# Order of products and placement of operands at the turn into a Strassen-Winograd up projection

## The chip, the cores and the metric

The kernel runs on one core of one Trainium2 chip. The metric is device time in microseconds, the median of three runs; a profile of one further execution tells where the time lies.

## The reference

Two layers of a hybrid encoder over 16 meta tokens and 1024 frames, width 1024. The change lies between the output projection of the attention half and the gated feed-forward that follows it:

```python
h = h + jnp.concatenate([o_gla, o_fox], axis=-1) @ w_out[i]
h = h + conv_ffn(rms_norm(h, ffn_norm[i]), w_up[i], conv_w[i], conv_b[i], w_down[i])

def conv_ffn(x, w_up, conv_w, conv_b, w_down):
    h = x @ w_up                       # 1040 x 1024 by 1024 x 5632
    hp = jnp.pad(h, ((0, 0), (CONV_W - 1, 0), (0, 0)))
    hc = conv_b
    for j in range(CONV_W):            # causal depthwise conv of width 3
        hc = hc + hp[:, j:j + L] * conv_w[j]
    u, g = jnp.split(hc, 2, axis=-1)
    return (jax.nn.silu(g) * u) @ w_down
```

## The kernel before

Everything is fp32 to the accuracy of a split: each operand is a high part `hi` (cast by ScalarE to the matmul's rounded fp32) and a low part `lo` (the rest, by VectorE), and `mm3` issues three matmuls for each pair of blocks, on lines L216, L217 and L218: hi by hi, lo by hi, hi by lo. Activations are transposed: 128 features on the partitions, tokens along the row. Tokens are taken in two halves of 520 (layer 0) or 516 and 8 more (layer 1), `sl[0]` and `sl[1]`, each as two chunks of 260 or 258 columns.

`ffn_up` does the output projection and the up projection. In the first, `wout` runs over the eight feature blocks m for half 0 and then for half 1: matmuls into one of four two-bank PSUM tiles, the residual add on VectorE (L1095), a store of the result to `hm` from GpSimd's queue (L1096), a square on ScalarE (L1101) and its sum into `acc` (L1102). After the second block of half 1, `scale(0)` turns the sum of half 0 into the norm's factor (a matmul with ones into `ssq`, then L1074, two ScalarE activations in `rsqrt`, L273 to L275), and `first_operand(k)` scales and splits block k of half 0 (L1079, and L1037 and L1038 in `put`); the table `turn` says after which block of half 1 which k are done.

The up projection multiplies each of 22 pairs j (128 columns of u, 128 of g) by the Strassen-Winograd scheme: features 0 to 511 and 512 to 1023 and the two halves of tokens form a 2 by 2 block problem with seven products p. A product is four k-blocks by two chunks by three matmuls, 24 in all. Products 1 and 2 use the first operands (k 0 to 3, and k 4 to 7) and need only half 0. Product 6 needs the operand T2, 7 needs T3, 4 needs N4, 5 needs T1, and 3 the fourth block itself; these are made from the residual stream, `dd`, and the norm's factor of half 1 by `make_t23`, `make_n4`, `make_t1` and `make_b22`, which the table `before` calls ahead of the i-th product of the order `seq`. Their sums are on VectorE (L1132, L1133, L1151) and GpSimd (L1144, L1152). `seq` starts with products 1 and 2 of pairs 0, 1 and 2, then runs 6, 7, 4, 5, 3 of pairs 0 and 1 alternately, and from pair 2 on one pair at a time.

On the weight side, `up_operand` loads the four half tiles A11, A12 (buffers `raw`, four of them, shared with the output projection) and A21, A22 (buffers `raw2`, seven) on SP's queue (L991; L983 for the first two products of pair 2), and VectorE combines them (L997): S1 = A21 + A22, S2 = S1 - A11, A21 = A11 - A21, A12 = A12 - S2. `up_split` casts (L1013) and subtracts (L1014). `ensure(i)` keeps the weights four products ahead (`AHEAD`).

In PSUM, product 1 lies in bank p0, p1 or p3 for pairs 0, 1 and 2, product 2 in p2 for all three; products 6, 7 and 4 go on accumulating in the bank of product 1. `evacuate` copies a bank out by ScalarE (L1181) or adds it by VectorE to what is there (L1180); after product 3 come the convolution (L1169, L1173), SiLU, the product of both (L1202) and a store from GpSimd's queue (L1203).

TensorE runs in the order in which the program is written (`manual_schedule`). The other engines' and queues' orders are fixed when the program is built, by a planner that takes what is ready by its own costs, the earliest traced first; each engine then runs its list in order. A buffer is taken again when its last reader is done.

Of the kernel before, what the change touches and what calls it, by code (L numbers as in the profile page):

```python
# [10 lines left out]
F32 = mybir.dt.float32  # L11
# [3 lines left out]
ALU = mybir.AluOpType  # L15
# [33 lines left out]
HALVES, HALVES_LAST = (0, 520, 520), (8, 524, 516)  # L49
AHEAD = 4  # L50
NSPLIT = 4


class Slots:
# [6 lines left out]
    def add(self, pool, n, prefix):  # L61
        ids = [(pool, f"{prefix}{i}") for i in range(n)]
        self.free += ids
        return ids
# [68 lines left out]
class Kern:  # L133
# [845 lines left out]
    def up_operand(self, lyr, j, p, fw, raws, odd):  # L979
        nc = self.nc  # L980
        if j == 2 and p in (1, 2):
            src = fw.tile([128, 4, 128], F32, tag="raw2", name="raw2")
            nc.sync.dma_start(src[:], self.wm[lyr, M_UP + 4][:, 4 * p - 4:4 * p, :])  # L983
            return self.up_split(src, fw, odd)
        if j not in raws:
            u, g = self.wm[lyr, M_UP + 2 * j], self.wm[lyr, M_UP + 2 * j + 1]
            q = raws[j] = {}
            for name, src, k0, own in (("A11", u, 0, True), ("A21", g, 0, False), ("A22", g, 4, False), ("A12", u, 4, True)):
                q[name] = self.wp.tile([128, 4, 128], F32, tag="raw", name="raw", bufs=4) if own else \
                    fw.tile([128, 4, 128], F32, tag="raw2", name="raw2")  # L990
                nc.sync.dma_start(q[name][:], src[:, k0:k0 + 4, :])  # L991
        q = raws[j]

        def combine(out, a, b, op):
            if out not in q:
                q[out] = fw.tile([128, 4, 128], F32, tag="raw2", name="raw2")
            nc.vector.tensor_tensor(out=q[out][:], in0=q[a][:], in1=q[b][:], op=op)  # L997
        if p == 6:
            combine("S1", "A21", "A22", ALU.add)
            combine("S2", "S1", "A11", ALU.subtract)  # L1000
        elif p == 7:
            combine("A21", "A11", "A21", ALU.subtract)
        elif p == 3:
            combine("A12", "A12", "S2", ALU.subtract)
        src = q[{1: "A11", 2: "A12", 3: "A12", 4: "A22", 5: "S1", 6: "S2", 7: "A21"}[p]]
        return self.up_split(src, fw, odd)
# [10 lines left out]
    def ffn_up(self, lyr, mix, hT, pp, fw, halves, o0, during_last):  # L1017
        nc, s = self.nc, self.slots
        W = halves[2]
        n = W // 2  # L1020
        sl = [slice(c, c + W) for c in halves[:2]]
        gain = lambda k: self.v(lyr, V_FN, k)
        bank2 = lambda name, i: pp.tile([128, 2, 512], F32, tag=f"p{i}", name=name, bufs=1)
        used = lambda ps: ps[:, :, :n]
        two = lambda ap: ap.rearrange("p (a b) -> p a b", b=n)
# [6 lines left out]
        def operand(x):  # L1032
            X[x] = [[s.get(F32R, f"x{x}", (128, 2, 520)) for _ in range(2)] for _ in range(2)]

        def put(x, k, src, lo=None):
            hi_, lo_ = (X[x][i][k // 2].t[:, k % 2, :W] for i in range(2))
            nc.scalar.copy(hi_, src)  # L1037
            (lo or nc.vector).tensor_tensor(out=lo_, in0=src, in1=hi_.bitcast(F32), op=ALU.subtract)  # L1038

        seq = [(j, p) for j in range(3) for p in (1, 2)] + [(j, p) for p in (6, 7, 4, 5, 3) for j in range(2)]
        seq += [(2, 6), (2, 5), (2, 7), (3, 1), (2, 4), (2, 3)]
        for j in range(3, NFF - 1):
            seq += [(j, 2), (j, 6), (j, 5), (j, 7), (j + 1, 1), (j, 4), (j, 3)]
# [15 lines left out]
        acc, sq = s.get(F32, "r"), half_slot("sq")  # L1061
# [15 lines left out]
        def first_operand(k):  # L1077
            h = hT[k][:, sl[0]]
            nc.vector.scalar_tensor_tensor(out=h, in0=h, scalar=gain(k), in1=acc[:, sl[0]], op0=ALU.mult, op1=ALU.mult)  # L1079
            put(1 + k // 4, k % 4, h)  # L1080
        turn = {1: (), 3: (0, 1), 4: (2,), 5: (3, 4), 6: (5,), 7: (6, 7)}

        def wout(i, h):
            m = orders[h][i]
            k0 = KD - 1 if m < NSPLIT else 0

            def f(w):
                if h == 1 and i == KD - 1:
                    ensure(0)
                ps = bank2("wo", i % 4)  # L1090
                for k in range(len(w)):
                    for c in range(2):
                        self.mm3(ps[:, c, :n], w[k], mix[k0 + k], halves[h] + c * n, n, k == 0, k == len(w) - 1)
                x = hT[m][:, sl[h]]
                nc.vector.tensor_tensor(out=two(x), in0=used(ps), in1=two(x), op=ALU.add)  # L1095
                nc.gpsimd.dma_start(self.hm[m][:, sl[h]], x)  # L1096
                if i == 0:
                    nc.scalar.activation(acc[:, sl[h]], x, AF.Square)
                else:
                    t = half(sq, i % 2)  # L1100
                    nc.scalar.activation(t, x, AF.Square)  # L1101
                    (nc.vector if h and i > 5 else nc.gpsimd).tensor_tensor(out=acc[:, sl[h]], in0=acc[:, sl[h]], in1=t, op=ALU.add)  # L1102
                if h == 0:
                    return
                if m < NSPLIT:
                    nc.scalar.mul(half(gt, m % 2), x, gain(m))
                else:
                    nc.vector.scalar_tensor_tensor(out=diff(m - 4), in0=x, scalar=gain(m), in1=half(gt, m % 2),
                                                   op0=ALU.mult, op1=ALU.subtract)
                if i == 1:  # L1110
                    scale(0)
                    operand(1)
                    operand(2)
                for k in turn.get(i, ()):
                    first_operand(k)
            return (self.wm[lyr, M_WO + m][:, k0:KD, :], f)
# [5 lines left out]
        lowk, highk, t0, t1 = hT[:4], hT[4:], sl[0], sl[1]  # L1122
# [2 lines left out]
            scale(1)  # L1125
            s.put(sq, *tmp)

        def make_t23():
            operand(6)
            for k in range(4):  # L1130
                x, y = diff(k), lowk[k][:, t0]
                nc.vector.tensor_tensor(out=x, in0=x, in1=acc[:, t1], op=ALU.mult)  # L1132
                nc.vector.tensor_tensor(out=y, in0=x, in1=y, op=ALU.add)  # L1133
                put(6, k, y)
            operand(7)
            for k in range(4):
                put(7, k, diff(k))
            s.put(*dd)

        def make_n4():  # L1140
            operand(4)
            for k in range(4):
                x = highk[k][:, t0]
                nc.gpsimd.tensor_tensor(out=x, in0=x, in1=lowk[k][:, t0], op=ALU.subtract)  # L1144
                put(4, k, x)

        def make_t1():
            operand(5)
            for k in range(4):
                x, y = highk[k][:, t1], lowk[k][:, t0]  # L1150
                nc.vector.scalar_tensor_tensor(out=x, in0=x, scalar=gain(4 + k), in1=acc[:, t1], op0=ALU.mult, op1=ALU.mult)  # L1151
                nc.gpsimd.tensor_tensor(out=y, in0=x, in1=y, op=ALU.subtract)  # L1152
                put(5, k, y)
            s.put(acc, *lowk)

        def make_b22():
            operand(3)
            for k in range(4):
                put(3, k, highk[k][:, t1])
            s.put(*highk)  # L1160
        before = {1: second_half, 2: make_t23, 7: make_n4, 9: make_t1, 12: make_b22}


        st = {}
# [13 lines left out]
        def evacuate(j, p):  # L1178
            q = st[j]
            add = lambda out, ps: nc.vector.tensor_tensor(out=two(out), in0=used(ps), in1=two(out), op=ALU.add)  # L1180
            copy = lambda out: nc.scalar.copy(two(out), used(q["a"]))  # L1181
            if p == 1:
                q["u"] = s.get(F32, "hu")
                copy(q["u"][:, t0])
            elif p == 6:
                copy(q["u"][:, t1])
            elif p == 7:
                q["g"] = s.get(F32, "hg")
                copy(q["g"][:, t1])
            elif p == 4:  # L1190
                copy(q["g"][:, t0])
            elif p == 2:
                add(q["u"][:, t0], q["y"])
            elif p == 3:
                add(q["u"][:, t1], q["x"])
                u, g = conv(q["u"], j), conv(q["g"], j + NFF)
                uo, go = u[:, o0:T], g[:, o0:T]
                nc.scalar.activation(go, go, AF.Silu)
                if j == NFF - 1:
                    self.preload = self.tc.keep_in_program_order(  # L1200
                        nc.scalar.preload_act_table_set("natural_log_exp_and_others"))
                nc.vector.tensor_tensor(out=uo, in0=uo, in1=go, op=ALU.mult)  # L1202
                nc.gpsimd.dma_start(self.actd[j][:, o0:T], uo)  # L1203
                s.put(u, g)
                del st[j]
            q.setdefault("done", set()).add(p)
            if p in (5, 7) and {5, 7} <= q["done"]:
                add(q["g"][:, t1], q["x"])

        for i, (j, p) in enumerate(seq):  # L1210
# [3 lines left out]
            q = st.setdefault(j, {})  # L1214
            bank, first = {2: "y", 5: "x", 3: "x"}.get(p, "a"), p in (1, 2, 5)
# [218 lines left out]
```

## Time and profile before

| | us |
|---|---|
| Runs | 2645.58, 2647.34, 3453.82 (median 2647.34) |
| Profiled execution | 2645.09 |
| its span | 2643.3 |
| TensorE busy | 2523.9 (95%) |
| VectorE busy | 1759.9 (67%) |
| ScalarE busy | 1240.1 (47%) |
| GpSimd busy | 457.9 (17%) |
| mean granted clock of TensorE | 0.987 |

In the profile PE is TensorE, PEld its weight loads, DVE VectorE, ACT ScalarE, POOL GpSimd, SP SyncE. A group's row has the line, engine, operation, tiles written and read, shapes and count, then busy time and mean nanoseconds of one, then the engine's idle time ahead of them and what ended it. A row of a timeline has start, length, the instruction, and in brackets the idle time before it with its releaser. Where several equal instructions follow each other, the row has them together. A window's row ends with the granted clock of TensorE, the mean busy share of the DMA engines, and GB/s. Output and up projection of layer 0 run from 550 us on, those of layer 1 from 1859 us on.

### The profile page before, as it was taken

To read this page: it belongs to the slowest core of one execution; us is meant where nothing else is said; L and a number is where in the kernel's file an instruction comes from. 1 tells how busy PE (TensorE), PEld (TensorE's weight loads), DVE (VectorE), ACT (ScalarE), POOL (GpSimd) and SP (SyncE) were. 2 spreads that over 40 slices of the span, in tenths; PEclk is the share of its full clock that TensorE was granted. 3 is DMA by queue.
4 is the path that set the end of the run, shared out by engine and by line. 5 is a ranking of instruction groups with operands and counts; after the bars stand their busy time and mean duration, and the time that the engine had idled before them with its cause. 6 is when DMAs were issued, how large, how long until landed. Compare 5 with 4: busy or idle time off the path is not lost.

```text
span 2643.3 us, 46336 instructions
## 1 busy us (share of the span) xinstructions
PE 2523.9 (95%) x18102; PEld 2407.2 (91%) x18102; DVE 1759.9 (67%) x3484; ACT 1240.1 (47%) x2677; POOL 457.9 (17%) x596
## 2 busy tenths in 40 slices
PE   8999999897999999999999999998989999999997
PEld 7988898897999999999999888887889999998886
DVE  7655676759877777643665666666698767776335
ACT  6345665645544445421343565665455444453112
POOL 4033333333000000000201333332320000000002
PEclk9999999998999999999999999999999999999999
DMA  3222124341222222632312222142512222245222
GB/s 125 65 83 70 47 83 124 106 131 58 97 81 76 85 77 92 217 94 58 103 56 65 75 72 74 56 138 91 158 51 85 83 81 77 83 139 189 65 55 77
DMA packets 114476, 240.72 MB, mean 91 GB/s; under 512 B 14432, under 2 KB 36192, under 8 KB 114256
## 3 DMA queue, kind: packets, MB, share of 16 engines
q1 hardware_dynamic: 96000, 182.27, 22.7%
q0 software_dynamic: 16384, 53.18, 5.5%
q8 instruction: 142, 2.33, 0.4%
q10 hardware_dynamic: 1872, 2.31, 0.2%
q14 instruction: 78, 0.64, 0.1%
HBM read 174.01 MB, written 50.91 MB: 85 GB/s over the span
## 4 chain that ended last, share of the span: by engine, by line
PE 77%; DVE 13%; ACT 4%; issue 3%; DMA 2%; POOL 2%; DVEq 0%; SPq 0%; POOLq 0%; ACTq 0%
PE mm L216 12%; PE mm L217 12%; PE mm L218 12%; PE up L216 10%; PE up L217 10%; PE up L218 10%; PE av L706 2%; PE tr L688 2%; DVE S L655 1%; DVE x L1038 1%; PE wo L217 1%; PE wo L216 1%; PE wo L218 1%; DVE PT L331 1%; ACT P L667 1%
## 5 line engine op out<-in xcount | busy, mean ns | idle before, releaser
L216 PE MATMUL up<-x,hi 128*128 128x260 f32 (+1 forms) x2464 | 701.3, 285 | 22.7 <-DVE hu L1180 20.3
L217 PE MATMUL up<-x,lo 128*128 128x260 f32 (+1 forms) x2464 | 699.2, 284 | 0.0
L218 PE MATMUL up<-x,hi 128*128 128x260 f32 (+1 forms) x2464 | 698.5, 283 | 0.0
L216 PEld LDWEIGHTS up<-x,hi 128*128 128x128 f32 x2464 | 467.5, 190 | 24.4 <-DVE hu L1180 20.7
L217 PEld LDWEIGHTS up<-x,lo 128*128 128x128 f32 x2464 | 467.9, 190 | 0.1
L218 PEld LDWEIGHTS up<-x,hi 128*128 128x128 f32 x2464 | 467.8, 190 | 0.0
L216 PE MATMUL mm<-xh,hi 128*128 128x348 f32 (+4 forms) x1056 | 365.1, 346 | 0.0
L218 PE MATMUL mm<-xl,hi 128*128 128x348 f32 (+4 forms) x1056 | 340.9, 323 | 0.0
L217 PE MATMUL mm<-xh,lo 128*128 128x348 f32 (+4 forms) x1056 | 340.8, 323 | 0.0
L1014 DVE TENSOR_TENSOR lo<-raw,hi 128x512 fp32r<-128x512 f32 x308 | 212.9, 694 | 146.2 <-ACT hi L1013 146.2
L183 ACT CAST hi<-raw 128x512 fp32r<-128x512 f32 (+1 forms) x264 | 142.3, 543 | 329.8 <-PE mm L218 240.0
L217 PE MATMUL mm<-ah,lo 128*128 128x400 f32 (+1 forms) x760 | 266.4, 351 | 0.2 <-DVE lo L185 0.2
L218 PE MATMUL mm<-al,hi 128*128 128x400 f32 (+1 forms) x760 | 265.9, 350 | 0.0
L216 PE MATMUL mm<-ah,hi 128*128 128x400 f32 (+1 forms) x760 | 265.8, 350 | 0.0
L185 DVE TENSOR_TENSOR lo<-raw,hi 128x512 fp32r<-128x512 f32 (+1 forms) x196 | 120.7, 620 | 181.1 <-ACT hi L183 177.5
L1013 ACT CAST hi<-raw 128x512 fp32r<-128x512 f32 x308 | 190.3, 620 | 107.6 <-PE up L218 92.7
L216 PEld LDWEIGHTS mm<-xh,hi 128*128 128x128 f32 x1056 | 201.0, 190 | 6.0 <-issue 5.3
L217 PEld LDWEIGHTS mm<-xh,lo 128*128 128x128 f32 x1056 | 200.9, 190 | 0.4 <-issue 0.3
L218 PEld LDWEIGHTS mm<-xl,hi 128*128 128x128 f32 x1056 | 199.9, 189 | 0.4 <-issue 0.3
L1203 POOL DMA_DIRECT2D actd<-cv x44 | 23.4, 533 | 830.0 <-DVE cv L1202 830.0
L667 ACT ACTIVATE P<-S,m 116x460 f32<-116x460 f32 (+2 forms) x224 | 124.8, 561 | 76.9 <-DVE m L655 72.6
L331 DVE TENSOR_TENSOR PT<-tr,PT 116x464 fp32r<-116x464 f32 (+3 forms) x240 | 122.1, 516 | 55.8 <-ACT PT L330 54.1
(248 smaller groups left out, 5269.0 us busy)
## 6 DMA issues: line engine op xcount, KB each, us to landing
raw<-in_wm_dram SPq DMA_DIRECT2D x328, 256.0 KB, 2.6
raw<-in_wd_dram SPq DMA_DIRECT2D x64, 256.0 KB, 2.6
actd<-cv POOLq DMA_DIRECT2D x22, 520.0 KB, 2.9
st<-actd SPq DMA_DIRECT2D x22, 520.0 KB, 4.9
actd<-cv POOLq DMA_DIRECT2D x22, 512.0 KB, 3.0
st<-actd SPq DMA_DIRECT2D x22, 512.0 KB, 4.8
cb<-cd SPq DMA_DIRECT2D x16, 520.0 KB, 4.2
kA<-kA SPq DMA_DIRECT2D x24, 260.0 KB, 3.8
```

The lines of the kernel that those rows point to most:

```text
L183: nc.scalar.copy(hi[:, :n, :], raw[:, :n, :])
L185: eng.tensor_tensor(out=lo[:, :n, :], in0=raw[:, :n, :], in1=hi[:, :n, :].bitcast(F32), op=ALU.subtract)
L216: nc.tensor.matmul(ps, wh, xh[:, c0:c0 + n], start=first, stop=False, skip_group_check=more)
L217: nc.tensor.matmul(ps, wl, xh[:, c0:c0 + n], start=False, stop=False, skip_group_check=more)
L218: nc.tensor.matmul(ps, wh, xl[:, c0:c0 + n], start=False, stop=last, skip_group_check=more)
L331: nc.vector.tensor_tensor(out=lo, in0=src, in1=hi.bitcast(F32), op=ALU.subtract)
L655: nc.vector.tensor_tensor_reduce(out=S[:rows, :n], in0=S[:rows, :n], in1=cb[:rows, c0:k1], scale=1.0, scalar=(BIG if ci == 0 else m[:rows, ...
L667: nc.scalar.activation(P[:rows, :n], S[:rows, :n], AF.Exp, scale=-1.0, bias=m[:rows, nch - 1:nch], accum_out=(den if nch == 1 else d3[:row ...
L688: nc.tensor.transpose(tr[:w, j, :rows], P[:rows, o:o + w], id_)
L706: nc.tensor.matmul(av[:, a:width], w.rearrange("p a b -> p (a b)"), x, start=(t == 0 and i == 0), stop=(t == last and i == 1))
L1013: nc.scalar.copy(hi[:], src[:])
L1014: nc.vector.tensor_tensor(out=lo[:], in0=src[:], in1=hi[:].bitcast(F32), op=ALU.subtract)
```

## The change

- In the first three pairs product 2 comes before product 1. The first product of a pair is copied to `u` by ScalarE, the second is added to it by VectorE. For pairs 3 to 21 the order stays.
- `turn` makes the first operands of k 4 to 7 before those of k 0 to 3.
- `make_t23` is parted: T2 stays at its place, behind the scale of half 1; T3 is traced ahead of the eighth product, N4 one product later than it was, T1 one product later too.
- The sums of squares (L1102) and the subtractions for N4 and T1 (L1144, L1152) are on VectorE in all cases.
- For pairs 0 to 4, S1 is not added by VectorE: A21's half tile is loaded once more into a `raw2` buffer of its own on SP's queue, as soon as the pair's tiles are, and a DMA from GpSimd's queue adds A22's half to it.

```diff
+N_DMA_SUM = 5
...
                 nc.sync.dma_start(q[name][:], src[:, k0:k0 + 4, :])
+            if j < N_DMA_SUM:
+                q["S1"] = fw.tile([128, 4, 128], F32, tag="raw2", name="raw2")
+                nc.sync.dma_start(q["S1"][:], g[:, 0:4, :])
+                nc.gpsimd.dma_start(q["S1"][:], g[:, 4:8, :], accum_op=ALU.add)
...
-            combine("S1", "A21", "A22", ALU.add)
+            if "S1" not in q:
+                combine("S1", "A21", "A22", ALU.add)
...
-        seq = [(j, p) for j in range(3) for p in (1, 2)] + [(j, p) for p in (6, 7, 4, 5, 3) for j in range(2)]
+        seq = [(j, p) for j in range(3) for p in (2, 1)] + [(j, p) for p in (6, 7, 4, 5, 3) for j in range(2)]
...
-        turn = {1: (), 3: (0, 1), 4: (2,), 5: (3, 4), 6: (5,), 7: (6, 7)}
+        turn = {1: (), 3: (4, 5), 4: (6,), 5: (7, 0), 6: (1,), 7: (2, 3)}
...
-                    (nc.vector if h and i > 5 else nc.gpsimd).tensor_tensor(out=acc[:, sl[h]], in0=acc[:, sl[h]], in1=t, op=ALU.add)
+                    nc.vector.tensor_tensor(out=acc[:, sl[h]], in0=acc[:, sl[h]], in1=t, op=ALU.add)
...
-        def make_t23():
+        def make_t2():
...
+        def make_t3():
             operand(7)
...
-                nc.gpsimd.tensor_tensor(out=x, in0=x, in1=lowk[k][:, t0], op=ALU.subtract)
+                nc.vector.tensor_tensor(out=x, in0=x, in1=lowk[k][:, t0], op=ALU.subtract)
...
-                nc.gpsimd.tensor_tensor(out=y, in0=x, in1=y, op=ALU.subtract)
+                nc.vector.tensor_tensor(out=y, in0=x, in1=y, op=ALU.subtract)
...
-        before = {1: second_half, 2: make_t23, 7: make_n4, 9: make_t1, 12: make_b22}
+        before = {1: second_half, 2: make_t2, 7: make_t3, 8: make_n4, 10: make_t1, 12: make_b22}
...
-            copy = lambda out: nc.scalar.copy(two(out), used(q["a"]))
-            if p == 1:
-                q["u"] = s.get(F32, "hu")
-                copy(q["u"][:, t0])
+            copy = lambda out, bank="a": nc.scalar.copy(two(out), used(q[bank]))
+            if p in (1, 2):
+                bank = "a" if p == 1 else "y"
+                if "u" in q:
+                    add(q["u"][:, t0], q[bank])
+                else:
+                    q["u"] = s.get(F32, "hu")
+                    copy(q["u"][:, t0], bank)
...
-            elif p == 2:
-                add(q["u"][:, t0], q["y"])
```

## The prediction

> **What bounds the kernel now.** I read the page first, then TensorE's waits around the two turns from the output projection into the up projection (layer 0 near 550 to 700 us, layer 1 near 1910 to 2060), then the stages by windows, then the timelines of VectorE, ScalarE and GpSimd inside the turn of layer 0.
>
> ```profile
> span 2643.3 us, 46336 instructions
> ...
> PE 2523.9 (95%) x18102; PEld 2407.2 (91%) x18102; DVE 1759.9 (67%) x3484; ACT 1240.1 (47%) x2677; POOL 457.9 (17%) x596
> ...
> L216 PE MATMUL up<-x,hi 128*128 128x260 f32 (+1 forms) x2464 | 701.3, 285 | 22.7 <-DVE hu L1180 20.3
> ```
>
> TensorE idles 22.7 us in front of the up products, 20.3 of it behind VectorE's evacuation L1180. TensorE's waits name the places, the first three lines in layer 0, the last in layer 1:
>
> ```profile
> PE up L216 <- DVE hu L1180: 10.2, 1, 10.2
> PE wo L217 <- DVE lo L185: 2.1, 1, 2.1
> PE wo L216 <- ACT hi L183: 1.7, 1, 1.7
> ...
> PE up L216 <- DVE hu L1180: 10.0, 1, 10.0
> ```
>
> So there is one stall of 10 us per layer. Its neighbourhood by windows (columns: length, then busy time and count of PE, PEld, DVE, ACT, POOL, then granted clock, DMA share, GB/s):
>
> ```profile
> 601.70:612.50 10.80, 8.65 (x48) 8.45 (x49) 9.20 (x14) 5.47 (x10) 3.60 (x3) 0.68 0.28 98
> 612.50:628.30 15.80, 15.70 (x126) 15.20 (x125) 14.28 (x23) 7.82 (x14) 3.54 (x3) 1.00 0.10 35
> 628.30:638.40 10.10, 0.00 (x0) 0.00 (x0) 8.98 (x12) 6.09 (x11) 4.36 (x3) 0.61 0.00 1
> 638.40:644.10 5.70, 5.64 (x26) 5.64 (x27) 4.87 (x10) 1.18 (x3) 0.00 (x0) 0.50 0.35 99
> 644.10:668.40 24.30, 23.25 (x192) 22.92 (x191) 24.27 (x33) 12.32 (x22) 6.72 (x4) 1.00 0.20 64
> ...
> 690.00:1068.00 378.00, 378.00 (x3155) 377.80 (x3154) 282.55 (x358) 188.75 (x269) 10.10 (x19) 1.00 0.27 90
> ```
>
> A product is 24 matmuls; 378 us over 3155 gives 0.120 us each, 2.88 us a product. Five products (120 matmuls and a norm sum) end by 628.3. Then come 10.1 us of nothing, and the sixth, product 2 of pair 2, needs 5.7 us because the clock is at 0.50: the stall costs 10.1 + 2.8. The next 192 matmuls, eight products, end at 668.4, where product 3 of pair 0 begins. From 690 on TensorE is full. VectorE is full as well, but only in the turn:
>
> ```profile
> 578.00:704.00 126.00, 109.48 (x845) 107.31 (x844) 116.56 (x159) 67.69 (x110) 32.46 (x27) 0.92 0.27 90
> ...
> 704.00:1068.00 364.00, 364.00 (x3038) 363.80 (x3038) 268.86 (x340) 181.68 (x260) 9.57 (x18) 1.00 0.27 89
> ```
>
> VectorE: 93% busy from 578 to 704, 74% after. Its timeline shows why the evacuation was late:
>
> ```profile
> 622.08 0.70 DVE L275 SCALAR_TENSOR_TENSOR r<-nt 128x520 f32<-128x520 f32 x1
> 622.69 0.69 DVE L997 TENSOR_TENSOR raw<-raw,raw 128x512 f32<-128x512 f32 x1
> 623.30 1.31 DVE L1132 TENSOR_TENSOR dd<-dd,r 128x520 f32<-128x520 f32 x2
> ...
> 626.35 0.69 DVE L1038 TENSOR_TENSOR x<-h,x 128x520 fp32r<-128x520 f32 x1
> 629.42 0.70 DVE L1038 TENSOR_TENSOR x<-h,x 128x520 fp32r<-128x520 f32 x1 [2.38 <-ACT x L1037]
> ...
> 637.71 0.69 DVE L1180 TENSOR_TENSOR hu<-up,hu 128x520 f32<-128x520 f32 x1
> 638.32 0.68 DVE L1014 TENSOR_TENSOR lo<-raw,hi 128x512 fp32r<-128x512 f32 x1
> 638.92 1.28 DVE L997 TENSOR_TENSOR raw<-raw,raw 128x512 f32<-128x512 f32 x2
> ```
>
> L1180 of product 2 of pair 1 (its matmuls ended by 625.4) stands in the queue behind T2 and T3 and runs at 637.71; bank p2 is free then and no sooner. In the middle VectorE idles 2.38 us for a ScalarE cast which itself sits behind GpSimd's subtraction:
>
> ```profile
> 628.24 1.15 ACT L1037 CAST x<-h 128x520 fp32r<-128x520 f32 x2 [2.36 <-POOL h L1144]
> ```
>
> **The change, part by part.** Instructions first. Two VectorE operations in a row take 1.31 us and one 0.70, so one more in a row costs 0.61.
>
> (a) *Product 2 ahead of product 1.* Product 2 now fills bank p2 and ScalarE copies it out; the add on VectorE is of product 1, in banks 0, 1 and 3, which product 6 of the same pair needs next. The three p2 products wait for copies (0.59 us, and ScalarE idles here), so the 10.1 us wait at the sixth product goes, with its half clock. Six products and the norm sum end at 628.3 + 2.9 = 631.2 and not 644.1: 12.9 us earlier. What is late next: product 6 of pair 0 needs T2, its weights S2, and the add of product 1.
>
> (b) *T2 alone.* r is ready at 622.8 (L275). T2 is 12 operations of VectorE, 7.3 us, and a cast of 0.62: about 631, plus three others that fall in between (a weight split, S2, one add), 1.8: 632.8 for the fourth piece, which product 6 wants at 631.2 + 2.2 = 633.4. No stall, or one of about 1 us. T3 and N4 stand behind and have one product and three products more.
>
> (c) *No arithmetic on GpSimd.* Twelve sums of squares and eight subtractions per layer move to VectorE. GpSimd's groups, and VectorE's own in the turn (mean ns last before the bar):
>
> ```profile
> L1102 POOL TENSOR_TENSOR r<-r,sq 128x520 f32<-128x520 f32 x12 | 18.7, 1554 | 1.7 <-ACT sq L1101 1.4
> ...
> L1144 POOL TENSOR_TENSOR h<-h,h 128x520 f32<-128x520 f32 x4 | 7.4, 1848 | 14.4 <-DVE h L1133 14.4
> L1152 POOL TENSOR_TENSOR h<-h,h 128x520 f32<-128x520 f32 x4 | 6.7, 1702 | 14.1 <-DVE h L1151 14.1
> ...
> L1038 DVE TENSOR_TENSOR x<-h,x 128x520 fp32r<-128x520 f32 x18 | 13.2, 752 | 2.4 <-ACT x L1037 2.4
> L1014 DVE TENSOR_TENSOR lo<-raw,hi 128x512 fp32r<-128x512 f32 x15 | 11.3, 758 | 0.0
> L997 DVE TENSOR_TENSOR raw<-raw,raw 128x512 f32<-128x512 f32 x14 | 10.2, 762 | 0.0
> L1038 DVE TENSOR_TENSOR x<-dd,x 128x520 fp32r<-128x520 f32 x4 | 4.9, 1233 | 0.0
> L1151 DVE SCALAR_TENSOR_TENSOR h<-h,vec,r 128x520 f32<-128x520 f32 x4 | 3.9, 1016 | 0.0
> L1132 DVE TENSOR_TENSOR dd<-dd,r 128x520 f32<-128x520 f32 x4 | 2.7, 698 | 0.0
> ```
>
> Where GpSimd computes, VectorE's operations of 0.70 us are stretched: against the 698 ns of L1132 (which ran with GpSimd idle) L1038 on dd loses 4 x 0.53, L1151 4 x 0.32, the other three groups 18, 15 and 14 times 0.06: 6.2 us in all, against 8 x 0.61 = 4.9 that the subtractions add there. So VectorE's turn gets no longer (bounds: 6.2 saved if they hid elsewhere, 4.9 lost if the stretching stays). The sum below counts every operation at its unstretched 0.61. In the projection itself 12 x 0.61 = 7.3 is added, seven of these while VectorE has idle time, and about as much stretching goes: 0 (bounds -3 to +3 of TensorE time, since the waits on lo L185 and hi L183 sit there).
>
> (d) *S1 by DMA.* Five adds of 0.61 per layer leave VectorE. One of them lay in idle time, two in the turn's busy stretch: 1.2 us. In their place come five loads on SP and five accumulating DMAs on GpSimd's queue, which first waits for the load; behind it stand only hm and actd stores that nobody waits for soon. No accumulating DMA is in this trace. Nearest rows:
>
> ```profile
> raw<-in_wm_dram SPq DMA_DIRECT2D x30, 256.0 KB, 2.7
> hm<-h POOLq DMA_DIRECT2D x14, 260.0 KB, 2.5
> ...
> st<-actd SPq DMA_DIRECT2D x22, 520.0 KB, 4.9
> ```
>
> A GpSimd-issued plain DMA of this size lands in 2.5; read, add and write back is at most two such passes, bounds 2.5 to 4.9. I take 4. S1 is then there 7 us after its buffer is free. For pairs 0 and 1 that is near 550, 60 us ahead of need. For pair 2 the buffer is free at the latest when product 4 of pair 1 starts, 631.2 + 5 x 2.88 = 645.6; S1 is there by 652.6, S2's weights 2 us later, and product 6 of pair 2 comes two products after the 656.6 worked out below, at 662.4: hidden, with 8 us to spare, for pairs 3 and 4 likewise.
>
> The ring of seven raw2 buffers is what (d) strains: two pairs hold A21, A22 and S1, six buffers, from the start; pair 2's two half loads and S2 of pair 0 pass one after the other through the seventh. The even split before the up products frees it here:
>
> ```profile
> 613.47 0.69 DVE L1014 TENSOR_TENSOR lo<-raw,hi 128x512 fp32r<-128x512 f32 x1
> ```
>
> so 614.2, load 2.7, cast 0.62, lo 0.7: 618.5; S2, cast and lo 2.0 more: 620 to 625 with queueing, against 631.2. Hidden, with 6 us to spare.
>
> **Sum.** From r at 622.8 to the last piece of T1, VectorE has T2 12, T3 4, N4 8, T1 12, two adds and 9 weight operations: 47 x 0.61 = 28.7, with 1.5 idle: 653.0. TensorE would like product 5 of pair 0 at 631.2 + 6 x 2.88 = 648.5 and its fourth piece at 650.7: 2.3 us late. Product 3 of pair 0 then begins at 648.5 + 2.3 + 5.8 = 656.6, not 668.4: 11.8 us won. VectorE's order outside TensorE is the planner's, fixed at build time; 637.71 shows it can put an urgent add 12 us late, and the convolutions follow at once on a full VectorE. For that I take back 3.3: 8.5 us per layer, 17 for both. Most this stage can give is no stall at all, 631.2 + 8 x 2.88 = 654.2: 14.2 per layer. 2645.1 (span 2643.3 and 1.8 around it) - 17 = **2628 us**. The median of the runs shown, 2647.3, stands 0.1% above the profiled execution, their lowest 2645.6.
>
> The clock could weigh in. In the 601.70 row waits of 1.7 and 2.1 us with a matmul between them, no more, already brought the clock to 0.68. The Trainium skill, TensorE: Matmul & The Clock Gate (Why this matters for your kernels), says that gaps up to about 3 us leave the clock alone; by that the 2.3 us stall above stays 2.3. By the row it could cost 3 more per layer and the sum would be 2634. The row decides, and the 3.3 taken back covers it.
>
> **Rivals.**
> *The wait moves.* Product 6 or 7 waits for T2, T3 or the add of product 1, because the planner interleaves N4 as it did before (the cast at 628.24). For: the 12 us delay of L1180. Against: N4 is later in program order and no longer slow. A stall of 8 us at half clock for one product leaves 2 to 3 us per layer: 2641.
> *More is won.* The projection's last tile also goes quickly: 10.8 us in the 601.70 row for 48 matmuls worth 5.8, and 1.7 before. With GpSimd silent, up to 6.7 more per layer, with 11.8: 2645 - 37 = 2608. Against: VectorE gets the sums of squares there.
> *Slower: the seventh raw2 buffer.* If the planner puts the low split of pair 2's second half load behind T2, T3 and N4, as it put L1014 at 638.32 (whose cast was ready at 624), that block is 15 us plus N4's eight operations, 4.9, from 622.7: 642.6. Then S2, cast, lo: 645. Product 6 starts at 645 after over 10 us of idle, at half clock: 648 where 644 was, 4 us lost, and with T1 then bunched another 4: 2645 + 16 = 2661. It decides if that split comes later than about 638. Against: it stands ahead of T2 in program order.
> *The DMA saves nothing.* S1's adds were in slack: 2 us less gain per layer, 2632, inside my range.
>
> **Chances.** Forecast 0.55, wait moves 0.2, more 0.12, slower 0.13. The range 2610 to 2652 leaves out the far part of the last two. A change of 2%, 53 us, is about what a measurement of this kernel can tell from none; the largest gain worked out is 37 and the largest loss 16, so faster 0.01, same 0.97, slower 0.02.
>
> **What would show it.** Right: no TensorE wait on hu L1180 over 3 us near 628; clock 1.00 from 625 to 650; L1038, L1151 and L1079 near 0.7 to 0.75 on VectorE; GpSimd with DMA issues only; product 3 of pair 0 begins 7 to 14 us sooner. Wrong: a wait over 5 us in front of any of the first 16 products, on T2's x, on raw, or on a landing of S1; or the projection's last tile longer than 12 us.

## The result, and the profile after

2628.78 us median (2625.91 to 2633.7) against 2647.34; the ratio is 0.993, 95% interval 0.9918 to 0.9942, so 15 to 22 us faster. One execution of `before` took 3453.82 us; without it the median there would be 2646.46. The profiled execution spans 2629.3 us, before 2643.3.

The page after (line numbers moved: the helper's matmuls are L217, L218 and L219 now, the casts and low parts of operands L1043 and L1044, of weights L1019 and L1020, the adds from PSUM L1188, T1's sums L1159 and L1160):

```profile
span 2629.3 us, 46309 instructions
...
PE 2526.3 (96%) x18102; PEld 2407.3 (92%) x18102; DVE 1751.8 (67%) x3514; ACT 1241.9 (47%) x2677; POOL 402.9 (15%) x566
...
L217 PE MATMUL up<-x,hi 128*128 128x260 f32 (+1 forms) x2464 | 698.9, 284 | 2.3 <-ACT x L1043 1.6
L219 PE MATMUL up<-x,hi 128*128 128x260 f32 (+1 forms) x2464 | 697.8, 283 | 1.9 <-DVE x L1044 1.8
L218 PE MATMUL up<-x,lo 128*128 128x260 f32 (+1 forms) x2464 | 697.5, 283 | 0.8 <-DVE lo L1020 0.8
```

The 22.7 us idle in front of the up products are 5.0 now, in three rows. Most of what is left waits for parts of an operand (x) or of a weight (lo); of the evacuations, one wait of 0.7 us (hg, layer 1) stands. VectorE has 30 instructions more and 8 us less to do. TensorE's waits around the turn of layer 0:

```profile
PE wo L218 <- DVE lo L186: 3.5, 2, 3.2
PE wo L217 <- DVE nt L1080: 1.9, 1, 1.9
PE up L217 <- ACT x L1043: 1.2, 2, 0.8
PE up L219 <- DVE x L1044: 0.7, 1, 0.7
```

And the stages (columns as in the windows of before):

```profile
612.50:631.30 18.80, 18.38 (x151) 18.09 (x149) 18.02 (x30) 11.60 (x21) 0.54 (x1) 1.00 0.18 52
631.30:648.50 17.20, 17.20 (x147) 17.20 (x146) 17.20 (x29) 10.51 (x19) 0.90 (x1) 1.00 0.41 114
648.50:660.20 11.70, 9.69 (x50) 8.71 (x49) 9.95 (x17) 4.57 (x8) 0.89 (x1) 0.71 0.26 67
660.20:704.00 43.80, 43.80 (x368) 43.80 (x367) 40.08 (x50) 26.38 (x36) 2.54 (x4) 1.00 0.37 119
```

Six products with 0.4 us idle in all (at the norm sum), six more without a stall, then two products in 11.7 us where 5.8 would do, with the clock at 0.71: that is where T1 is awaited. Product 3 of pair 0 begins at 660.2, before at 668.4.

For the experiments one number of the trace serves best, the length of the up projection, from its first matmul to its last: 459.4 us in layer 0 and 459.8 in layer 1 before, 450.0 and 450.5 after, 18.7 won in both. The rest of the kernel is the same in both, but its time is not quite: from the end of layer 0's up projection to layer 1's first output-projection matmul 787.2 us passed before and 790.7 after, and in the profiles of all fourteen kernels between 784.4 and 791.9. This is most of why the profiled executions differ by 14.0 and not by 18.7, and why one execution's total tells little within some 4 us here.

### The profile page after: what moved, and what is told of

Read it like the earlier page. It is cut to its first block, busy times and chain, and to the rows that moved or that the text cites. A ratio compares the mean times of both kernels' runs of the same rounds, so it can differ in the third digit from the quotient of the medians.

```text
span 2629.3 us, 46309 instructions
## 1 busy us (share of the span) xinstructions
PE 2526.3 (96%) x18102; PEld 2407.3 (92%) x18102; DVE 1751.8 (67%) x3514; ACT 1241.9 (47%) x2677; POOL 402.9 (15%) x566
## 4 chain that ended last, share of the span: by engine, by line
PE 76%; DVE 12%; issue 4%; ACT 4%; DMA 2%; POOL 1%; SPq 0%; DVEq 0%; POOLq 0%; ACTq 0%
PE mm L217 12%; PE mm L218 12%; PE mm L219 12%; PE up L217 9%; PE up L219 9%; PE up L218 9%; PE av L707 2%; PE tr L689 2%; DVE S L656 2%; PE wo L217 1%; PE wo L218 1%; PE wo L219 1%; DVE PT L332 1%; DVE x L1044 1%; DMA cb<-cd 1%
## 5 line engine op out<-in xcount | busy, mean ns | idle before, releaser
L217 PE MATMUL up<-x,hi 128*128 128x260 f32 (+1 forms) x2464 | 698.9, 284 | 2.3 <-ACT x L1043 1.6
L219 PE MATMUL up<-x,hi 128*128 128x260 f32 (+1 forms) x2464 | 697.8, 283 | 1.9 <-DVE x L1044 1.8
L218 PE MATMUL up<-x,lo 128*128 128x260 f32 (+1 forms) x2464 | 697.5, 283 | 0.8 <-DVE lo L1020 0.8
L219 PEld LDWEIGHTS up<-x,hi 128*128 128x128 f32 x2464 | 466.5, 189 | 2.9 <-DVE x L1044 2.9
L217 PEld LDWEIGHTS up<-x,hi 128*128 128x128 f32 x2464 | 465.9, 189 | 3.5 <-ACT x L1043 2.2
L218 PEld LDWEIGHTS up<-x,lo 128*128 128x128 f32 x2464 | 466.3, 189 | 1.0 <-DVE lo L1020 1.0
L217 PE MATMUL mm<-xh,hi 128*128 128x348 f32 (+4 forms) x1056 | 365.2, 346 | 0.0
L218 PE MATMUL mm<-xh,lo 128*128 128x348 f32 (+4 forms) x1056 | 340.9, 323 | 0.0
L219 PE MATMUL mm<-xl,hi 128*128 128x348 f32 (+4 forms) x1056 | 340.7, 323 | 0.0
L1020 DVE TENSOR_TENSOR lo<-raw,hi 128x512 fp32r<-128x512 f32 x308 | 210.1, 686 | 140.2 <-ACT hi L1019 140.2
L218 PE MATMUL mm<-ah,lo 128*128 128x400 f32 (+1 forms) x760 | 266.5, 351 | 0.9 <-DVE lo L186 0.9
L219 PE MATMUL mm<-al,hi 128*128 128x400 f32 (+1 forms) x760 | 265.4, 349 | 0.0
L217 PE MATMUL mm<-ah,hi 128*128 128x400 f32 (+1 forms) x760 | 265.4, 349 | 0.0
L1019 ACT CAST hi<-raw 128x512 fp32r<-128x512 f32 x308 | 190.3, 621 | 113.8 <-PE up L219 87.2
L186 DVE TENSOR_TENSOR lo<-raw,hi 128x512 fp32r<-128x512 f32 (+1 forms) x196 | 110.8, 569 | 175.3 <-ACT hi L184 171.6
L217 PEld LDWEIGHTS mm<-xh,hi 128*128 128x128 f32 x1056 | 201.0, 190 | 6.0 <-issue 5.3
L218 PEld LDWEIGHTS mm<-xh,lo 128*128 128x128 f32 x1056 | 200.9, 190 | 0.4 <-issue 0.3
L219 PEld LDWEIGHTS mm<-xl,hi 128*128 128x128 f32 x1056 | 199.8, 189 | 0.4 <-issue 0.3
L218 PEld LDWEIGHTS mm<-ah,lo 128*128 128x128 f32 x760 | 142.8, 188 | 14.6 <-DVE lo L186 1.5
```

The costliest lines, as they stand in the source:

```text
L186: eng.tensor_tensor(out=lo[:, :n, :], in0=raw[:, :n, :], in1=hi[:, :n, :].bitcast(F32), op=ALU.subtract)
L217: nc.tensor.matmul(ps, wh, xh[:, c0:c0 + n], start=first, stop=False, skip_group_check=more)
L218: nc.tensor.matmul(ps, wl, xh[:, c0:c0 + n], start=False, stop=False, skip_group_check=more)
L219: nc.tensor.matmul(ps, wh, xl[:, c0:c0 + n], start=False, stop=last, skip_group_check=more)
L1019: nc.scalar.copy(hi[:], src[:])
L1020: nc.vector.tensor_tensor(out=lo[:], in0=src[:], in1=hi[:].bitcast(F32), op=ALU.subtract)
```

## The experiments

Theory A: the wait for bank p2 is what costs, and the new order removes it. Theory B: VectorE's queue limits the turn; GpSimd's subtractions stretch it and hold it up, and the order of products decides only where the wait falls.

Each entry gives the median time, its ratio to runs of `before` taken beside it (medians 2644.68 to 2648.72) with the 95% interval, and the length of the up projection in layers 0 and 1, from one profile.

**order_only**: `before`, with `seq`, `turn` and `evacuate` of the change (the first two are shown).

```diff
-        seq = [(j, p) for j in range(3) for p in (1, 2)] + ...
+        seq = [(j, p) for j in range(3) for p in (2, 1)] + ...
-        turn = {1: (), 3: (0, 1), 4: (2,), 5: (3, 4), 6: (5,), 7: (6, 7)}
+        turn = {1: (), 3: (4, 5), 4: (6,), 5: (7, 0), 6: (1,), 7: (2, 3)}
```

> Only the order of products 1 and 2 in three pairs, with the operands' turn and the evacuation that go with it; T2 and T3 together, GpSimd arithmetic and S1 by VectorE as before. Theory A (the wait for bank p2 is what costs, and the order alone removes it): no wait of TensorE near the sixth product, up projection of a layer 459.4 us before, about 451 then, total about 2628. Theory B (the turn is limited by VectorE's queue, which GpSimd's subtractions stretch and hold up; the order alone only moves the wait to T2): product 6 of pair 0 waits for x near 634 to 637, about 4 us and half clock for a product, up projection 454 to 456, total 2635 to 2640.

2644.63 us, ratio 0.9999 (0.9988 to 1.001); up projection 458.7 and 459.2. Nothing is gained. Its waits in layer 0, and the stage from product 6 of pair 0 to the end of product 6 of pair 1:

```profile
PE up L218 <- DVE x L1038: 2.8, 2, 1.8
PE up L216 <- ACT hg L1181: 2.7, 1, 2.7
PE up L216 <- ACT hi L1013: 2.4, 1, 2.4
```

```profile
635.30:645.40 10.10, 4.37 (x27) 3.44 (x25) 10.10 (x14) 5.34 (x11) 3.27 (x2) 0.80 0.00 0
645.40:651.70 6.30, 5.73 (x25) 5.43 (x26) 5.27 (x9) 0.90 (x2) 0.00 (x0) 0.51 0.41 127
```

The sixth product runs at once, and product 6 of pair 0 then takes 10.1 us, VectorE busy throughout, the next one 6.3 at half clock. The stall has moved by one product. Theory A falls; B's own figures for this run (a wait of about 4 us, 454 to 456) were missed as well.

**vector_only**: `before`, with sums of squares and subtractions on VectorE.

```diff
-(nc.vector if h and i > 5 else nc.gpsimd).tensor_tensor(out=acc[:, sl[h]], ...
+nc.vector.tensor_tensor(out=acc[:, sl[h]], ...
-nc.gpsimd.tensor_tensor(out=x, in0=x, in1=lowk[k][:, t0], op=ALU.subtract)
+nc.vector.tensor_tensor(out=x, in0=x, in1=lowk[k][:, t0], op=ALU.subtract)
-nc.gpsimd.tensor_tensor(out=y, in0=x, in1=y, op=ALU.subtract)
+nc.vector.tensor_tensor(out=y, in0=x, in1=y, op=ALU.subtract)
```

> Only the arithmetic moved from GpSimd to VectorE (sums of squares, subtractions of N4 and T1); old order, T2 and T3 together, S1 by VectorE. Theory A: the sixth product still waits for the add of product 2 of pair 1 behind T2 and T3; that add comes at about 633 instead of 637.7, so 4 us less wait per layer, up projection about 455, total about 2637. Theory B: as much as that or more, since the whole queue of VectorE is shorter until T1: up projection 450 to 453, total 2628 to 2633.

2630.31 us, ratio 0.9948 (0.9929 to 0.9966); 453.1 and 452.7, at the upper end of B's 450 to 453. The old wait still stands, shortened:

```profile
PE up L216 <- DVE hu L1180: 5.7, 1, 5.7
```

**after_old_order**: the changed kernel with `seq` and `turn` of before (the first two lines of the first diff, reversed).

> The changed kernel with product 1 ahead of product 2 again and the old turn. Theory A: most of the gain is lost, a wait of 5 us or more at the sixth product, up projection 455 or more, total about 2637. Theory B: the add stands directly behind T2 (12 operations) since T3 is later, at about 631; a wait of about 3 us at the sixth product, half of which comes off the wait for T1 later: up projection 450 to 452, total about 2630.

2630.54 us, 0.9948 (0.9933 to 0.9963); 449.8 and 450.1, as with the new order. The wait at the sixth product is 3.4 us in layer 0 and 1.5 in layer 1, where the new order has none, and the later waits cost as much less. The order is worth nothing with the other parts either.

**after_s1_vector**: the changed kernel without accumulating DMAs.

```diff
-N_DMA_SUM = 5
+N_DMA_SUM = 0
```

> The changed kernel with S1 added by VectorE for all pairs (no accumulating DMA). Both theories: two adds of 0.61 us more in the turn's busy stretch, so at most 1.2 us longer wait for T1 per layer: up projection 450 to 452, total 2628 to 2632. If the DMA is the main thing, over 2634.

2623.64 us, 0.9924 (0.9904 to 0.9944); 450.1 and 452.2, where the changed kernel has 450.0 and 450.5. The total lies under the 2628 to 2632 that were expected; this profile has the 784.4 us between the layers, the shortest of all. In layer 1 the first up product takes 4.9 us with the norm sum, in the changed kernel 3.8, which is 1.1 of the 1.7: the norm's matmul waits there for the last sum of squares, at full clock.

```profile
PE ssq L1077 <- DVE r L1108: 1.1, 1, 1.1
```

S1 by DMA brings nothing that shows.

**after_subs_gpsimd**: the changed kernel with the subtractions on GpSimd (the last two pairs of lines of the second diff, reversed).

> The changed kernel with the eight subtractions for N4 and T1 back on GpSimd; sums of squares stay on VectorE. Theory B (VectorE's queue up to T1 sets the length, and GpSimd's subtractions stretch it and hold up ScalarE's casts): T1 late by 4 to 6 us more, up projection 454 to 457 per layer against 450, total 2637 to 2642. Rival C (the gain of the vector arithmetic came from the sums of squares, that is from the operands of the first half being ready sooner): up projection stays near 450, total about 2629.

2638.57 us, 0.9968 (0.9955 to 0.9981); 454.5 and 454.5, as B had it (454 to 457): 4.2 of the 9.4 us per layer are lost. VectorE waits in the turn for a cast that itself waits 4.2 us for GpSimd's subtraction, as it did before:

```profile
DVE x L1044 <- ACT x L1043: 3.7, 1, 3.7
```

**after_squares_gpsimd**: the changed kernel with the sums of squares on GpSimd, as before (the first pair of lines of the second diff, reversed).

> The changed kernel with ten of the sums of squares per layer... that is all but the last two of half 1, back on GpSimd; subtractions stay on VectorE. Theory B: up projection unchanged at 450, output projection 61 to 62.5 us as in both kernels, total 2627 to 2631. Rival C: up projection 454 or more or the output projection over 1 us longer, total 2635 to 2640.

2626.46 us, 0.9925 (0.9908 to 0.9943); 448.7 and 450.1. Nothing is lost: rival C falls, the subtractions are the arithmetic that counts.

**after_t3_with_t2**: the changed kernel with T3 made right behind T2.

```diff
-        before = {1: second_half, 2: make_t2, 7: make_t3, 8: make_n4, 10: make_t1, 12: make_b22}
+        before = {1: second_half, 2: lambda: (make_t2(), make_t3()), 8: make_n4, 10: make_t1, 12: make_b22}
```

> The changed kernel with T3 made directly behind T2 again, ahead of the third product. If parting T3 off is worth something beside the vector arithmetic: T3's four low parts, 2.4 us, come ahead of the add of product 1 and of product 6's weights, so product 6 or 7 waits 1 to 3 us (perhaps with half clock), up projection 451 to 454. If VectorE's total up to T1 alone counts: 450, since the operations are the same and the wait at T1 shrinks by what came before.

2628.67 us, 0.9932 (0.9917 to 0.9947); 447.5 in layer 0, 452.9 in layer 1. In layer 1 a wait of 2.4 us comes up (for the cast of a weight, L1019), and the clock is halved for one stretch around it; in layer 0 neither.

```profile
PE up L217 <- ACT hi L1019: 2.4, 1, 2.4
```

On the mean, 450.2, no loss shows: here T3 need not be apart from T2. N4 and T1 stay at their later places in this run.

**early_2_6**: a version of the changed kernel that gives T1 one product more of time.

```diff
-... for p in (6, 7, 4, 5, 3) for j in range(2)]
-        seq += [(2, 6), (2, 5),
+... for p in (6, 7, 4) for j in range(2)]
+        seq += [(2, 6)] + [(j, p) for p in (5, 3) for j in range(2)] + [(2, 5),
-        before = {..., 12: make_b22}
+        before = {..., 13: make_b22}
```

> A version of the changed kernel with product 6 of pair 2 moved ahead of product 5 of pair 0, so that T1 has one product more of time. Theory B: T1 is due 2.9 us later, and VectorE has two operations more before it (1.2 us): the wait at product 5, 3.9 us, falls to about 2 and the half clock behind it (2.0) may go: up projection 446 to 449, total 2620 to 2627. Rival: the weights of product 6 of pair 2 are late, since S1 of pair 2 and a free buffer for S2 come only after product 5's weights are split: a wait of 2 us or more there instead, up projection 450 or more.

2630.99 us, 0.9941 (0.9921 to 0.996); 449.6 and 449.2, above the 446 to 449 that Theory B had here. The wait at T1 is down to 0.5 us in layer 0 and gone in layer 1. But in layer 0 VectorE stands for S1 by DMA, and product 4 of pair 0, which needs N4, then takes 5.9 us:

```profile
DVE raw L1002 <- DMA raw<-in_wm_dram: 2.8, 1, 2.8
```

**early_2_6_s1_vector**: the same with S1 on VectorE and the sums of squares on GpSimd.

```diff
-N_DMA_SUM = 5
+N_DMA_SUM = 0
-nc.vector.tensor_tensor(out=acc[:, sl[h]], ...
+(nc.vector if h and i > 5 else nc.gpsimd).tensor_tensor(out=acc[:, sl[h]], ...
```

> The version with product 6 of pair 2 ahead of product 5 of pair 0, now with S1 by VectorE for all pairs and all but two of half 1's sums of squares on GpSimd again. With S1 by DMA VectorE stood 2.8 us for pair 2's S1 there; without that wait and with 0.6 us for each add instead: wait at T1 1 to 2 us, no half clock, up projection 446 to 447.5, total 2618 to 2624. Rival: the wait is VectorE's total, and an earlier product does not shorten it: 449 to 450, total 2626 to 2630.

2632.01 us, 0.9937 (0.9916 to 0.9959); 449.4 and 450.3. Without the DMA wait the time is the same: TensorE now waits in two places, 1.4 and 1.2 us, for an add to hg.

```profile
PE up L217 <- DVE hg L1188: 2.5, 2, 1.4
```

The length is the rival's (449 to 450): an earlier product does not shorten it. The rival's reason, VectorE's total, fits, but this run does not show it apart.

**subs_only**: `before`, with the two subtractions (`x` and `y` in the second diff) on VectorE.

> The kernel before with the eight subtractions for N4 and T1 per layer on VectorE and nothing else (two words of the source). Theory B: nearly all of the gain, up projection 452 to 454 per layer against 459.4, total 2630 to 2634, with a wait of 5 to 6 us still standing at the sixth product. Rival D (several parts must come together): 456 or more, total over 2637.

2637.25 us, 0.9957 (0.9943 to 0.9971); 451.8 and 453.8. By the length, Theory B's 452 to 454, two words of the source give 6.8 of the 9.4 us per layer; the total is above B's 2630 to 2634, at the edge of rival D's. The 5.6 us at the sixth product are as expected:

```profile
PE up L216 <- DVE hu L1180: 5.6, 1, 5.6
```

VectorE's groups in the stretch of its turn:

```profile
L1038 DVE TENSOR_TENSOR x<-h,x 128x520 fp32r<-128x520 f32 x18 | 12.0, 692 | 0.0
L1151 DVE SCALAR_TENSOR_TENSOR h<-h,vec,r 128x520 f32<-128x520 f32 x4 | 2.9, 750 | 0.0
L1152 DVE TENSOR_TENSOR h<-h,h 128x520 f32<-128x520 f32 x4 | 2.7, 690 | 0.0
```

Before, L1038 had 752 ns and 2.4 us idle, L1151 1016 ns. And the add that bank p2 waited for:

```profile
631.64 0.69 DVE L1180 TENSOR_TENSOR hu<-up,hu 128x520 f32<-128x520 f32 x1
```

In this run the up projection begins at 611.1, in the profile of before at 612.6; so the add comes 20.5 us behind the begin, not 25.1.

**order_and_subs**: the subtractions together with the new order.

> The same two subtractions together with the new order of products, operands' turn and evacuation; T2 and T3 together, squares and S1 as before the change. If the order adds to the subtractions once VectorE is relieved: 3 us per layer below the subtractions alone, up projection about 450, total 2624 to 2629. If the order only moves the wait: within 1 us of the subtractions alone, 452 to 454.

2636.5 us, 0.9946 (0.9928 to 0.9965); 451.2 and 454.1, 0.2 less on the mean than the subtractions alone. The order only moves the wait.

**subs_t3_apart**: `before`, with the subtractions and with T3, N4 and T1 traced later.

```diff
-        before = {1: second_half, 2: make_t23, 7: make_n4, 9: make_t1, 12: make_b22}
+        before = {1: second_half, 2: make_t2, 7: make_t3, 8: make_n4, 10: make_t1, 12: make_b22}
```

> The kernel before with two of the change's parts: the eight subtractions on VectorE, and T3, N4 and T1 traced later as in the change. Old order of products, sums of squares and S1 as before. If these two parts are the whole effect: up projection about 450 per layer as with the full change, total 2626 to 2632. If the last 2.5 us per layer need S1 by DMA or the order as well: 452 to 453.5, as with the subtractions alone, total 2632 to 2637.

2630.66 us, 0.9939 (0.9917 to 0.996); 449.8 and 451.0. The old wait at the sixth product is now

```profile
PE up L216 <- DVE hu L1182: 1.3, 1, 1.3
```

These two parts are the whole gain, as far as the trace can tell.

No version's interval lies clear of the changed kernel's on the faster side.

## Why the prediction was right, and where not

The time came out as forecast (2628 against 2628.8), by a sum that was right where it followed VectorE and credited a part that does nothing. That it is right to 0.8 us is luck: 17 us were taken from one execution of 2645.1, and the medians differ by 18.6, the profiled executions by 14.1.

**(a) The order: wrong cause.** That product 6 of pair 0 would begin at 631.2 was right; it began at 631.3, the end of the first window above. But the text gives the 12.9 us to the order. Alone the order brings 0.6 per layer and on top of the subtractions 0.2, and without it the other parts bring as much as with it (after_old_order). The rival "the wait moves" describes what it does by itself. The gain survived because the sum did not stop at 12.9: it asked when VectorE has T1 ready.

**(b) T2 alone: right in time.** The fourth low part of T2 was put at 632.8; it is the one at 631.97, which ends at 632.7, behind an add and a weight's split as reckoned:

```profile
631.37 0.69 DVE L1188 TENSOR_TENSOR hu<-up,hu 128x520 f32<-128x520 f32 x1
631.97 0.69 DVE L1044 TENSOR_TENSOR x<-h,x 128x520 fp32r<-128x520 f32 x1
```

Parting T3 off, with N4 and T1 one product later, counts for about 2.4 per layer in the old order (subs_t3_apart against subs_only).

**(c) No arithmetic on GpSimd: right, and undersold.** The stretched groups came down, L1044 on dd to where L1132 was:

```profile
L1159 DVE SCALAR_TENSOR_TENSOR h<-h,vec,r 128x520 f32<-128x520 f32 x4 | 2.9, 754 | 0.0
...
L1044 DVE TENSOR_TENSOR x<-dd,x 128x520 fp32r<-128x520 f32 x4 | 2.5, 696 | 0.0
```

L1159, the scalar form, came to 754; its like, L1108, had 752 to 758 in `before` already, so L1151 lost 0.26 each and not the 0.32 that the text took against L1132. Nor did all operations stretch a little, and two of the four L1132 did not run with GpSimd idle, as the text has it. Beside the subtraction at 630.88, L1132 kept its 0.70 and the instruction behind it took 1.78:

```profile
630.65 0.70 DVE L1132 TENSOR_TENSOR dd<-dd,r 128x520 f32<-128x520 f32 x1
631.26 1.78 DVE L1038 TENSOR_TENSOR x<-dd,x 128x520 fp32r<-128x520 f32 x1
```

```profile
630.88 1.61 POOL L1144 TENSOR_TENSOR h<-h,h 128x520 f32<-128x520 f32 x1 [1.43 <-DVE h L1133]
```

There are six such instructions in the turn of layer 0, of 1.77 to 1.81 us, which makes 6.6 us in all, near the 6.2 of the text.

The step priced this part at 6.2 saved against 4.9 added, 1.3 us. That is what the removed stretching brings; the idle time of VectorE behind casts that waited for GpSimd goes too, and the add in front of bank p2 comes earlier. That was in the sum, since it counts each operation at 0.61 with 1.5 us idle in all, but it was not named as this part's gain. By itself the part with the subtractions gives 6.8 of 9.4; the sums of squares give nothing that shows (vector_only, after_squares_gpsimd). In the output projection nothing changes, as expected (61.9 us before, 62.0 after in layer 0), so the rival by which more is won there falls too.

**(d) S1 by DMA: its price right, its gain not shown.** Four us were taken for the accumulating DMA; the trace from 536 to 690 has

```profile
raw<-in_wm_dram POOLq DMA_DIRECT2D x5, 256.0 KB, 4.3
```

Product 6 of pair 0 began without a wait, so the seventh raw2 buffer was no trouble there. Of the 1.2 us credited to this part nothing shows in layer 0 (after_s1_vector), as the rival of S1's adds in slack had it.

**The wait at T1: too small.** Product 5 of pair 0 began at 648.5 to the tenth, but took 6.8 us, not the 2.9 + 2.3 reckoned, because the last low part of T1 (the first of the two in the second row here) ended near 654.2 and not at 653.0, the third piece came late and not the fourth alone, and the clock was halved from 653.0 on:

```profile
651.07 0.69 DVE L1044 TENSOR_TENSOR x<-h,x 128x520 fp32r<-128x520 f32 x1
...
653.51 1.30 DVE L1044 TENSOR_TENSOR x<-h,x 128x520 fp32r<-128x520 f32 x2
```

The term of the sum that was off is the nine weight operations ahead of T1's last part: there were 13, and no idle time. Product 5 of pair 1 took 4.9 instead of 2.9 at the lowered clock. Product 3 then began 3.6 later than the 656.6 of the sum. The 3.3 us taken back, which the text says cover the clock, are near these 3.6, but they were put there for the planner's order, and their size comes from no row: this too is luck.

**The clock.** Of the two rules weighed, the row of the 601.70 window was the better guide. The Trainium skill, TensorE: Matmul & The Clock Gate (Why this matters for your kernels), allows gaps up to about 3 us. Here the longest single wait of an up product in the turn was 0.8 us, and the clock of the window 648.50:660.20 was 0.71. The trace of layer 0 does not agree. Waits of 0.4, 0.7 and 0.8 us stood in the one product there, and the clock was 0.50 behind them (first row). In layer 1 the same product waits 0.5, 0.4 and 0.7 us and the clock stays at 1.00 (second row), so what decides between the two is open:

```profile
653.10:659.80 6.70, 6.35 (x27) 6.05 (x28) 5.35 (x9) 0.83 (x2) 0.89 (x1) 0.50 0.40 106
1952.30:1961.20 8.90, 6.69 (x51) 5.86 (x49) 8.90 (x16) 5.25 (x10) 0.88 (x1) 1.00 0.30 78
```

**Left open.** Parting T3 off is worth 2.4 with the old order, together with the later places of N4 and T1, and nothing in after_t3_with_t2, where N4 and T1 keep those places. Whether T3's place counts at all, or whether the new order, S1 by DMA or the sums of squares make up for it there, was not tried apart.

## What to carry to other kernels

When an engine waits for a buffer, ask first whether the instruction that frees it is late because of its place or because its engine is full: here another order of products moved the wait, and what shortened it was time taken off the full engine (6.8 us) and operands that are needed later being made later (2.4 us). Work given to GpSimd can cost VectorE more than it takes over, as the 1.78 us instructions beside its subtractions show; look at single instructions and not only at the mean of a group. Test each part of a bundle alone, even when the forecast of the whole comes out right.

## What the runs showed that was not expected

Half clock needs no long gap: in layer 0 of the changed kernel, with waits of at most 0.8 us each strung through one product, the granted clock was 0.71 over 11.7 us, and the next product took 4.9 us. It does not always follow, as layer 1 shows. The two layers of after_t3_with_t2, in the same order of work, differ by 5.4 us in the up projection: 3.4 lie in the first 16 products, where the wait of 2.4 us and the half clock stand, and the rest behind them, where the layers of the changed kernel differ by 2.1 as well. An accumulating DMA of 256 KB takes 0.9 us of GpSimd's queue to issue, against 0.54 for a plain one of 260 KB:

```profile
614.22 0.54 POOL L1102 DMA_DIRECT2D hm<-h  x1 [6.92 <-DVE h L1101]
639.16 0.90 POOL L996 DMA_DIRECT2D raw<-in_wm_dram  x1 [24.40 <-DMA raw<-in_wm_dram]
```
